# One encoder layer on one NeuronCore: the output projection of the second half interleaved, the first attention operands loaded ahead of the last key stores, the last RWKV pair among the last projections

## The chip, the cores and the metric

The kernel runs on one core of one Trainium2 chip. The core has TensorE (PE in the profile; PEld is its weight load), VectorE (DVE), ScalarE (ACT), GpSimd (POOL) and SyncE (SP), whose queue issues nearly all DMAs here. The metric is the device time of one execution in microseconds (us). Lower is better.

## What is computed

One layer of a streaming encoder, in fp32, for a prompt of 1024 frames and a sample of 64 frames that continues a past of 256 frames. The reference, cut to its skeleton:

```python
mod = silu(c) @ w_ada + b_ada                      # 6 x 1024 per sequence
sh1, sc1, gt1, sh2, sc2, gt2 = split(mod, 6)
h = rms_norm(x, norm1_g) * (1 + sc1) + sh1
proj = h @ w_in                                    # 1792 RWKV columns, 1544 FoX columns
# RWKV-7 group, 8 heads x 64: gates, delta-rule scan over time, group norm, bonus, gate
y_rwkv = ((groupnorm(scan(r, decay, k, v, kk, a, s0)) + bonus) * g)
# forgetting attention, 8 heads x 64: q, k normed; bias = difference of cumulated log forget
s = q @ k.T * 64**-0.5 + lc_q - lc_k               # causal mask, softmax
y_fox = softmax(s) @ v
x = x + gt1 * (concat(y_rwkv, y_fox) @ w_out)
h2 = rms_norm(x, norm2_g) * (1 + sc2) + sh2
x = x + gt2 * ((silu(h2 @ w_gate) * (h2 @ w_up)) @ w_down)     # 2816 wide
```

The outputs are x for both sequences, the RWKV states and shift rows, and the keys, values and log forget values of the new frames.

## The kernel before

**Halves and tiles.** The 1088 columns (frames) are worked on in two halves, called 0 (512 prompt frames) and 1 (512 prompt frames and the 64 sample frames, 576 in all). Activations lie with features on the partitions. Every large product is done in three fp32r matmuls: a weight and an activation are each split into a high part (`whi`, a cast on ACT) and a low part (`wlo`, a subtraction on DVE or on POOL, chosen by `pool_lo`), and high x high, high x low and low x high are added in PSUM (`mm3`). The weights come through a ring (`rraw` with four buffers of 512 KB, `whi` and `wlo` with two each).

**The order.** The program is written in one order, which serves as priority. A planner in the tile framework then lays out each engine's queue by what it takes to be ready, so that the queues mix stages where it finds room. On the chip each queue goes in its fixed order. A tile that takes over the space of another waits for that one's last user.

**The stages:**

1. Conditioning: 48 tiles of `w_ada`, each eight small matmuls, a copy on ACT, a transpose and a reduction on DVE (`ada_mm`, `ada_fin`). The first 16 come before anything else, the other 32 are dealt out one per projection (`background`).
2. `phase` for half 0, then half 1, in the order of the string `ORDER`. Z, D, A, B and N are the steps of one of four RWKV head pairs: Z projects, A builds the chunk matrices, B (`rwkv_b`) inverts them and runs a chain of 8 or 9 chunks, N norms and stores. Q, K and V project, q and k norm and store to DRAM scratch (`qx`, `kx`, `vscr`; `put_split` does the key and query stores), C puts the cached keys there, L makes the log forget rows. A pair whose B or N is not in the string is done "late": half 0's pair 3 at T3 and U3 in half 1's string, half 1's pair 3 after the phase.
3. Attention (`attend`) of half 0, head after head, in units that are staggered by a pipeline (`Pipe`). Each head first loads its operands `qs`, `q2`, `k1`, `k2`, `vs` from the scratch into one of two sets of tiles, by eight or nine DMAs. The sets lie in the pool `attp` and are shared by both halves. Then attention of half 1, with the output projection of half 0 dealt out between heads (`outproj`, po in the trace).
4. Squares of half 0's residual (`x1_sq`), the norm (`x1_rs`) and the FFN's operands of half 0 (`h2_make`, all of it), then the eight output tiles of half 1, each with its square; from output 5 on the first pair of "gate" weights is loaded and, at 6, prepared (`fast_raw`, `fast_prep`); then the "up" pair is loaded, and half 1's norm made.
5. The FFN in 22 steps (a weight pair of gate, then of up) of two passes each, half 0 and half 1. A pass (`fast_half`) is a Strassen-like product of seven groups of 12 matmuls. Hooks after each group carry on the preparation of the next weights (`STEPS`), half 1's `h2_make` (in the first pass) and, in the last pass, `mid`: the loads and splits of the first activations for the down projection.
6. The down projection (`down`): six groups of activations, eight output tiles each, with a weight split per tile (48 in all) on POOL, since `pool_lo` is set to True ahead of attention.

In the order of the program, B3 and N3 of half 1 stand here, after the whole string, and the operand tiles are made after them in space that the phase's work tiles held:

```python
hst.close()
fxs.close()
for b, f in late.values():
    f(b())
```

## Time and profile before

| | us |
|---|---|
| median of 3 runs | 1759.51 |
| lowest, highest | 1754.32, 1764.12 |
| the profiled execution, as timed | 1761.91 |
| its span in the profile | 1760.2 |
| mean granted clock of TensorE | 0.974 |

The span runs from the first to the last instruction. Busy time of an engine is the time in which one of its instructions runs; matmuls overlap in the pipeline, so that a busy PE isn't PE at its peak. A row of a stage table gives the stretch, its length, the busy time of PE, PEld, DVE, ACT and POOL with their numbers of instructions, the granted clock of TensorE (1.00 is full speed), the busy share of the 16 DMA engines and GB/s. A row in order of time gives start, duration, engine, line, operation, tiles and the number of instructions merged into it; in square brackets stands how long the engine had been idle, and what released it. A row of a group gives line, engine, operation, tiles and number, busy time and the mean of one in ns, then idle time before it and what ended it. SPq is SyncE's queue of DMA issues.

### The profile page before, as it was taken

To read this page: it belongs to the slowest core of one execution; us is meant where nothing else is said; L and a number is where in the kernel's file an instruction comes from. 1 tells how busy PE (TensorE), PEld (TensorE's weight loads), DVE (VectorE), ACT (ScalarE), POOL (GpSimd) and SP (SyncE) were. 2 spreads that over 40 slices of the span, in tenths; PEclk is the share of its full clock that TensorE was granted. 3 is DMA by queue.
4 is the path that set the end of the run, shared out by engine and by line. 5 is a ranking of instruction groups with operands and counts; after the bars stand their busy time and mean duration, and the time that the engine had idled before them with its cause. 6 is when DMAs were issued, how large, how long until landed. Compare 5 with 4: busy or idle time off the path is not lost.

```text
span 1760.2 us, 33567 instructions
## 1 busy us (share of the span) xinstructions
PE 1673.6 (95%) x12893; PEld 1454.0 (83%) x12893; DVE 1105.8 (63%) x2518; ACT 728.0 (41%) x1532; POOL 267.6 (15%) x468
## 2 busy tenths in 40 slices
PE   5999999999999998889999779999999999999999
PEld 3676666688888886666888779999999999999998
DVE  6676676757786753777876685556666654444434
ACT  4435454543555344566776363233333222112110
POOL 2102121121222122100212300000000000222221
PEclk9999999999999997889999899999999999999999
DMA  8435356642233336376663302222222224533313
GB/s 314 151 87 157 116 165 195 184 122 71 76 75 92 107 84 167 96 203 166 158 188 128 106 34 83 74 74 74 74 74 78 79 89 134 182 99 93 99 36 120
DMA packets 136143, 207.10 MB, mean 118 GB/s; under 512 B 64687, under 2 KB 72911, under 8 KB 135983
## 3 DMA queue, kind: packets, MB, share of 16 engines
q1 hardware_dynamic: 135982, 204.95, 39.1%
q8 instruction: 102, 1.67, 0.4%
q14 instruction: 59, 0.48, 0.1%
HBM read 157.65 MB, written 47.25 MB: 116 GB/s over the span
## 4 chain that ended last, share of the span: by engine, by line
PE 81%; DVE 7%; ACT 6%; issue 3%; DMA 3%; POOL 1%; SPq 0%; ACTq 0%; DVEq 0%; POOLq 0%
PE pd L1244 15%; PE pfc L1143 7%; PE pfe L1143 7%; PE pfa L1143 7%; PE pmm L294 5%; PE pmm L296 5%; PE pmm L295 5%; PE pfb L1143 4%; PE pav L952 2%; PE pbs L375 2%; PE ppt L930 2%; PE pA L464 2%; PE pS L613 1%; PE po L295 1%; PE po L294 1%
## 5 line engine op out<-in xcount | busy, mean ns | idle before, releaser
L216 POOL TENSOR_TENSOR wlo<-wraw,whi 128x512 fp32r<-128x512 f32 (+2 forms) x64 | 107.1, 1675 | 777.5 <-ACT whi L212 772.2
L294 PE MATMUL pmm<-hhi,whi 128*128 128x288 f32 (+1 forms) x624 | 220.3, 353 | 1.0 <-ACT pb L317 0.7
L295 PE MATMUL pmm<-hlo,whi 128*128 128x288 f32 (+1 forms) x624 | 216.8, 347 | 1.4 <-DVE hlo L272 1.4
L296 PE MATMUL pmm<-hhi,wlo 128*128 128x288 f32 (+1 forms) x624 | 215.6, 345 | 0.0
L212 ACT CAST whi<-wraw 128x1024 fp32r<-128x1024 f32 (+2 forms) x116 | 99.2, 855 | 234.8 <-PE pd L1244 168.1
L1244 PE MATMUL pd<-ah,whi 128*128 128x512 f32 (+1 forms) x528 | 173.3, 329 | 2.2 <-ACT ah L212 2.2
L1244 PE MATMUL pd<-al,whi 128*128 128x512 f32 (+1 forms) x528 | 174.1, 330 | 0.5 <-DVE al L216 0.5
L1244 PE MATMUL pd<-ah,wlo 128*128 128x512 f32 (+1 forms) x528 | 173.7, 329 | 0.0
L1248 DVE SCALAR_TENSOR_TENSOR x1t<-pd,mod,x1t 128x512 f32<-128x512 f32 x192 | 90.6, 497 | 132.1 <-PE pd L1244 131.0
L294 PEld LDWEIGHTS pmm<-hhi,whi 128*128 128x128 f32 x624 | 119.2, 191 | 14.3 <-ACT pb L317 2.5
L295 PEld LDWEIGHTS pmm<-hlo,whi 128*128 128x128 f32 x624 | 119.4, 191 | 11.1 <-DVE hlo L272 2.1
L296 PEld LDWEIGHTS pmm<-hhi,wlo 128*128 128x128 f32 x624 | 119.4, 191 | 10.2 <-issue 1.2
L1143 PE MATMUL pfc<-hh,hS 128*128 128x256 f32 (+1 forms) x352 | 102.3, 291 | 8.0 <-ACT hh L1045 5.6
L1244 PEld LDWEIGHTS pd<-ah,whi 128*128 128x128 f32 x528 | 99.8, 189 | 10.5 <-ACT ah L212 2.7
L1244 PEld LDWEIGHTS pd<-al,whi 128*128 128x128 f32 x528 | 99.8, 189 | 8.5 <-DVE al L216 0.7
L1244 PEld LDWEIGHTS pd<-ah,wlo 128*128 128x128 f32 x528 | 99.9, 189 | 7.5
L604 POOL TENSOR_SCALAR sd<-sv,pc 64x64 f32<-64x64 f32 x136 | 72.1, 530 | 202.7 <-DVE sv L617 190.3
L1143 PE MATMUL pfc<-hl,hS 128*128 128x256 f32 (+1 forms) x352 | 102.4, 291 | 0.0
L1143 PE MATMUL pfc<-hh,lS 128*128 128x256 f32 (+1 forms) x352 | 102.2, 290 | 0.0
L1143 PE MATMUL pfa<-hh,whi 128*128 128x256 f32 (+1 forms) x352 | 102.0, 290 | 0.0
L1143 PE MATMUL pfa<-hl,whi 128*128 128x256 f32 (+1 forms) x352 | 101.8, 289 | 0.0
L1143 PE MATMUL pfa<-hh,wlo 128*128 128x256 f32 (+1 forms) x352 | 101.4, 288 | 0.0
(360 smaller groups left out, 4471.6 us busy)
## 6 DMA issues: line engine op xcount, KB each, us to landing
wraw<-in_w_in_dram SPq DMA_DIRECT2D x52, 512.0 KB
wada<-in_w_ada_dram SPq DMA_DIRECT2D x48, 512.0 KB
as<-actscr SPq DMA_DIRECT2D x22, 544.0 KB
wraw<-in_w_gate_dram SPq DMA_DIRECT2D x22, 512.0 KB
wraw<-in_w_up_dram SPq DMA_DIRECT2D x22, 512.0 KB
wraw<-in_w_down_dram SPq DMA_DIRECT2D x40, 256.0 KB
wraw<-in_w_out_dram SPq DMA_DIRECT2D x16, 512.0 KB
actscr<-sg SPq DMA_DIRECT2D x22, 288.0 KB
```

Source lines behind the costliest of these rows:

```text
L212: nc.scalar.copy(hi, src)
L216: eng.tensor_tensor(lo, src, hi.bitcast(F32), op=ALU.subtract)
L294: nc.tensor.matmul(ps[0:M, 0:n], whi[:, k, 0:M], xhi[:, k, off:off + n], start=(k == 0), stop=False)
L295: nc.tensor.matmul(ps[0:M, 0:n], whi[:, k, 0:M], xlo[:, k, off:off + n], start=False, stop=False)
L296: nc.tensor.matmul(ps[0:M, 0:n], wlo[:, k, 0:M], xhi[:, k, off:off + n], start=False, stop=(k == kt - 1))
L375: nc.tensor.matmul(ps[:, 0:n], w, x[:, off:off + n], start=True, stop=True)
L464: nc.tensor.matmul(pa[h][:, i], kb[hp, c + i], rk[hp, c + i], start=True, stop=True)
L604: nc.gpsimd.tensor_scalar(sd[hsl[h]], sv[hsl[h], c, h], pc[hsl[h], c], None, op0=ALU.mult)
L930: nc.tensor.transpose(pt[0:rows, b - b0, t * P:t * P + qn], p[0:qn, b * P:b * P + rows], self.ident[0:qn, 0:qn])
L1143: nc.tensor.matmul(ps, l[:, k], r[:, s, k], start=(first and k == 0 and y == 0), stop=(k == 3 and y == 2), skip_group_check=True)
L1244: nc.tensor.matmul(ps[:, 0:n], w[:, i], x[:, t:t + n], start=(i == 0 and y == 0), stop=(i == len(fs) - 1 and y == 2))
L1248: nc.vector.scalar_tensor_tensor(dst, ps[:, so - off:so - off + l], self.mod[:, 40 + o, b:b + 1], dst, op0=ALU.mult, op1=ALU.add)
```

## The change

- `ORDER` of half 1 gets `P B3` ahead of the last `K2 k3 k2 V3`. P closes the RWKV work pools (now a stack of their own, `rws`, on the left, while the attention side's pools `fxs` move to the right), makes operand tiles for half 0 in their place (`at0`) and issues the 16 loads of heads 0 and 1. B3 then runs in the phase; N3 stays late.
- Half 0 and half 1 have operand tiles of their own (`att_ops`, `att_load`).
- The sample's new keys stand ahead of its cached keys in `kx`, so that a half's 576 columns are stored by one DMA in place of two; mask and transposes follow that order.
- `pool_lo` is set to False ahead of the squares of half 0: the low parts of the weights in half 1's output projection and in the down projection are made on DVE.
- The first two `w_out` weights of half 1 are loaded and split ahead of half 0's `h2_make`, whose steps are dealt out between half 1's outputs.
- The conditioning tiles 40 to 47, needed only in the down projection, are taken from the projections: 40 to 43 run after half 1's outputs, 44 to 47 in `gap`, between half 0's and half 1's first pass. The "up" weights are loaded there too, and prepared during half 1's first pass.
- The activations 0 and 1 for the down projection are loaded one weight pair earlier (`early` in `ffn`), 2 and 3 at the start of the last pass.

The diff, cut to its core:

```diff
-         "... V0 Q2 q2 K3 N2 Q3 q3 K2 k3 k2 V3")
+         "... V0 Q2 q2 K3 N2 Q3 q3 P B3 K2 k3 k2 V3")
...
             for h in range(2):
                 t = (self.kx if is_k else self.qx)[2 * j + h, r:r + 64]
-                hs = slice(64 * h, 64 * h + 64)
-                nc.sync.dma_start(t[:, t0:t0 + m], x[hs, 0:m].bitcast(F32))
-                if n > m:
-                    c = SP + PAST if is_k else SP
-                    nc.sync.dma_start(t[:, c:c + SS], x[hs, 512:576].bitcast(F32))
+                nc.sync.dma_start(t[:, t0:t0 + n], x[64 * h:64 * h + 64, 0:n].bitcast(F32))
...
+    def att_ops(self, pools, hf):
+        nq, nk, nb = (640, SP + PAST + SS, 11) if hf.smp else (512, 512, 4)
+        ops = [[p.tile(s, F32R, name=f"{n}x{i}") for n, s in (("qs", [P, nq]), ("q2", [68, nq]), ("k1", [P, nk]),
+                                                               ("k2", [68, nk]), ("vs", [P, nb, P]))]
+               for i, p in enumerate(pools)]
...
+        self.ops[hf.i] = ops
...
+        if hd > 1 or hf.smp:
+            self.att_load(hd, hf)
...
-    def outproj(self, hf, o, tags=("mm",)):
-        wh, wl = self.load_w(self.A["w_out"][o], [P, KT, P])
+    def outproj(self, hf, o, tags=("mm",), w=None):
+        wh, wl = w or self.load_w(self.A["w_out"][o], [P, KT, P])
...
+                def prep(x):
+                    for _ in range((0, 0, 0, 3, 2, 2, 1)[x] if i == 0 else self.STEPS[hf.i][x]):
+                        next(gen, None)
...
                 if i == 0 and hf.i == 0:
                     for _ in h2gen:
                         pass
+                    gap()
+                    raw.append(self.fast_raw(src[2]))
+                    gen = self.fast_prep(raw[1], nw)
...
-            self.background = [lambda t=t: self.ada_fin(self.ada_mm(t)) for t in range(16, 48)]
+            self.background = [lambda t=t: self.ada_fin(self.ada_mm(t)) for t in range(16, 40)]
...
+            def early():
+                rws.close()
+                p = E(at0, "att0")
+                self.att_ops([p, p], halves[0])
+                for hd in range(2):
+                    self.att_load(hd, halves[0])
...
+            self.pool_lo = False
             acc = None
             for o in range(KT):
                 acc = self.x1_sq(halves[0], o, acc)
-            for _ in self.h2_make(halves[0], self.x1_rs(halves[0], acc)):
-                pass
+            w1 = [self.load_w(A["w_out"][o], [P, KT, P]) for o in range(2)]
+            h2 = self.h2_make(halves[0], self.x1_rs(halves[0], acc))
...
             for o in range(KT):
-                self.outproj(halves[1], o, ("ab", "ce")[o % 2])
+                self.outproj(halves[1], o, ("ab", "ce")[o % 2], w1[o] if o < 2 else None)
                 acc = self.x1_sq(halves[1], o, acc)
+                next(h2, None)
+                if o in (0, 2):
+                    next(h2, None)
+                if o == 4:
+                    raw.append(self.fast_raw(pair("w_gate")))
                 if o == 5:
-                    raw.append(self.fast_raw(pair("w_gate")))
-                if o == 6:
                     for _ in self.fast_prep(raw[0], w):
                         pass
-            raw.append(self.fast_raw(pair("w_up")))
+            for _ in h2:
+                pass
+            ada = [(t, self.ada_load(t)) for t in range(40, 44)]
             rs = self.x1_rs(halves[1], acc)
...
+            def gap():
+                ada_run(ada[4:])
+                raw.append(self.fast_raw(pair("w_up")))
+            ada_run(ada)
+            ada += [(t, self.ada_load(t)) for t in range(44, 48)]
...
+            def early():
+                h2s[2].close()
+                self.spool.pools["as"] = L(early_s, "sas0", 2)
+                for f in range(2):
+                    pre.append(self.act_load(f, None))
...
             def mid(x):
                 if x == 0:
...
-                if x in (0, 1):
-                    pre.append(self.act_load(x, apools[0]))
-                if x in (3, 4):
-                    pre[x - 3] = self.act_split(pre[x - 3])
-                    pre.append(self.act_load(x - 1, apools[0]))
...
+                    for f in range(2, 4):
+                        pre.append(self.act_load(f, None))
...
+                if 0 < x < 5:
+                    pre[x - 1] = self.act_split((pre[x - 1][0], apools[0]))
```

More of the change, by code (lines that the diff above doesn't have):

```diff
@@ L87, in consts @@
         nc.vector.reciprocal(sg, sg)
-        self.ct = self.cmid.tile([P, KT, 32], F32, name="ct")
+        self.ct = c.tile([P, KT, 32], F32, name="ct")
         nc.gpsimd.memset(self.ct, 0.0)
@@ L703, in logf @@
         if hf.smp:
-            order += [(5, True, SP, P, None), (6, False, SP + P, P, None), (4, False, SP + PAST, SS, SP)]
+            order += [(5, True, SP + SS, P, None), (6, False, SP + SS + P, P, None), (4, False, SP, SS, SP)]
         acc = self.lacc
@@ L852, in att_pools, with att_load @@
         nc.vector.tensor_copy(self.cmask, cm)
[L853 to L861 removed]
+    def att_ops(self, pools, hf):
[3 more added lines that the diff above has]
+               for i, p in enumerate(pools)]
+        if hf.smp:
+            for qs, q2, _, _, _ in ops:
+                for t in (qs, q2):
+                    self.nc.gpsimd.memset(t[:, 576:640].bitcast(F32), 0.0)
+        self.ops[hf.i] = ops
+    def att_load(self, hd, hf):
         nc = self.nc
[L864 to L867 removed]
+        qs, q2, k1, k2, vs = self.ops[hf.i][hd % 2]
         n, t0 = hf.n, hf.t0
@@ L906, in unit @@
                     c += w
-                nc.tensor.matmul(pq[0:qn, nk - qn:nk], self.identb[0:qn, 0:qn], self.cmask[0:qn, 0:qn], start=False,
+                cm = 0 if smp else nk - qn
+                nc.tensor.matmul(pq[0:qn, cm:cm + qn], self.identb[0:qn, 0:qn], self.cmask[0:qn, 0:qn], start=False,
                                  stop=True, skip_group_check=True)
@@ L1157, in fast_half, with ffn @@
                 h(x)
-    def ffn(self, halves, raw, w, h2gen, mid):
+    def ffn(self, halves, raw, w, h2gen, gap, early, mid):
         nc, A = self.nc, self.A
@@ L1168, in ffn @@
             p, up = i // 2, i % 2
-            if i + 2 < len(src):
+            if i and i + 2 < len(src):
                 raw.append(self.fast_raw(src[i + 2]))
+            if i == len(src) - 2:
+                early()
             old, nw = gen, {}
-            gen = self.fast_prep(raw[i + 1], nw) if i + 1 < len(src) else iter(())
+            gen = self.fast_prep(raw[i + 1], nw) if 0 < i < len(src) - 1 else iter(())
             for hf in halves:
@@ L1302, in phase @@
                 self.cache_kv(j)
+            elif op == "P":
+                self.early()
             elif op == "S":
@@ L1433, in run @@
             self.spool.pools.update({"fs": L(mix0, "sfs", 2)})
+            self.att_ops([R(att, f"attp{i}", 1) for i in range(2)], halves[1])
             PB = lambda es, name, b: E(es, name, b, space=PSUM, reuse_waits="tile")
```

87 lines of the change are left out of this document (46 added, 41 removed).

## The prediction

> **What bounds the kernel now.** I read the page first: the span, the busy shares and the chain that ended last.
>
> ```profile
> span 1760.2 us, 33567 instructions
> ...
> PE 1673.6 (95%) x12893; PEld 1454.0 (83%) x12893; DVE 1105.8 (63%) x2518; ACT 728.0 (41%) x1532; POOL 267.6 (15%) x468
> ...
> PE 81%; DVE 7%; ACT 6%; issue 3%; DMA 3%; POOL 1%; SPq 0%; ACTq 0%; DVEq 0%; POOLq 0%
> ```
>
> TensorE (PE) is busy for 95% of the span and makes up 81% of the chain, so only the holes in PE are worth anything, together with the slices in which its granted clock falls. Next I took the busy time by stage, with bounds that I set where the work changes. The columns are the stretch, its length, the busy time of PE, PEld, DVE, ACT and POOL, the granted clock, the DMA share and GB/s.
>
> ```profile
> 60.00:440.00 380.00, 366.97 (x3118) 273.60 (x3118) 263.51 (x728) 176.48 (x386) 69.09 (x156) 0.97 0.47 135
> ...
> 660.00:683.00 23.00, 22.73 (x297) 19.58 (x297) 8.85 (x15) 13.35 (x26) 5.19 (x5) 1.00 0.52 144
> 683.00:717.00 34.00, 26.05 (x157) 19.83 (x149) 10.54 (x39) 10.11 (x34) 7.03 (x18) 0.52 0.45 119
> 717.00:745.00 28.00, 25.83 (x148) 19.00 (x147) 22.84 (x73) 19.05 (x59) 5.64 (x20) 0.97 0.44 123
> 745.00:780.00 35.00, 28.62 (x166) 20.44 (x166) 28.84 (x88) 25.58 (x79) 3.91 (x20) 1.00 0.63 178
> 780.00:815.00 35.00, 30.05 (x129) 22.14 (x129) 21.98 (x43) 19.16 (x40) 0.34 (x2) 0.80 0.77 219
> ...
> 940.00:1011.00 71.00, 57.80 (x404) 56.05 (x404) 50.62 (x66) 34.09 (x47) 24.40 (x7) 0.93 0.41 134
> 1011.00:1035.00 24.00, 14.35 (x101) 12.95 (x101) 20.00 (x34) 22.04 (x35) 0.00 (x0) 0.95 0.03 13
> 1035.00:1480.00 445.00, 444.98 (x3514) 444.69 (x3514) 267.15 (x507) 135.99 (x253) 1.66 (x1) 0.99 0.24 75
> 1480.00:1500.00 20.00, 17.25 (x106) 15.76 (x105) 10.76 (x15) 6.43 (x7) 1.82 (x1) 0.92 0.89 292
> 1500.00:1757.00 257.00, 256.92 (x1555) 234.29 (x1553) 113.76 (x207) 44.47 (x63) 57.86 (x46) 1.00 0.32 101
> ```
>
> The FFN (1035 to 1480) and the down projection (1500 to 1757) are full and can give nothing. Four places are not: 683 to 780 (last RWKV pair, then attention of half 0), 940 to 1011 (output projection of half 1), 1011 to 1035 (norm of half 1) and 1480 to 1500 (turn to the down projection). The change works on just these.
>
> **Part 1: pair 3 of half 1 (B3) among the last projections, first attention operands loaded ahead.** I looked at the order of time on PE and on SP's queue.
>
> ```profile
> 624.58 0.46 PE L597 MATMUL pR<-sv,At 128*128 128x128 f32 x2
> ...
> 652.17 0.46 PE L597 MATMUL pR<-sv,At 128*128 128x128 f32 x2
> ...
> 679.35 0.59 PE L523 MATMUL pg<-gt,At 32*32 32x32 f32 x25
> ...
> 699.37 0.77 PE L597 MATMUL pR<-sv,At 128*128 128x128 f32 x2 [0.36 <-DVE sv L617]
> ...
> 703.65 0.77 PE L597 MATMUL pR<-sv,At 128*128 128x128 f32 x2 [0.36 <-DVE sv L617]
> ...
> 705.48 0.77 PE L902 MATMUL psc<-k1x,qsx 128*128 128x256 f32 x2
> ```
> ```profile
> 659.54 0.34 SPq L625 DMA_DIRECT2D out_state_s_dram<-state  x1
> ...
> 663.26 0.60 SPq L800 DMA_DIRECT2D qx<-shi  x1
> ...
> 692.36 0.42 SPq L870 DMA_DIRECT2D qsx<-qx  x1
> ```
>
> B3 begins at 679.35, when the projections are used up, and runs alone: one chunk takes 703.65 - 699.37 = 4.28 us, with a granted clock of 0.52. Pair 2, among projections, took (652.17 - 624.58) / 7 = 3.94 us for a chunk while PE was filled by other work. The loads for the first two attention heads are issued from 692.36 on, behind a row of stores of 0.6 us each, and the first score matmul comes at 705.48. After the change those 16 loads (eight a head) stand ahead of K2, k3, k2 and V3 and need only half 0's rows, long since written; the space they load into is that of the RWKV work tiles, whose last user is A3. B3 can begin once pair 2's state is out (659.54), with two projections left to fill its gaps, and attention once the last projection has read the activations, near 685.
>
> The worth by PE's work: 660 to 780 holds 22.73 + 26.05 x 0.52 + 25.83 + 28.62 = 90.7 us of PE at full clock. The 22.7 of projections run at the share of their row, 0.99. The other 68 run at the share of attention beside a chain (25.83 / 28 = 0.92), or at that of attention alone (28.62 / 35 = 0.82): 23 + 74 = 97 us or 23 + 83 = 106 us, for 120 now. So 14 to 23 us, and I take **18**, the middle, as both kinds of stretch remain. The low end for the range is 0 (attention starts where it did); a loss is excluded only if SP does not hold weight loads behind the 16 issues that come early, 16 x 0.6 = 10 us at worst. The 16 are moved, not added. The single store for 576 columns takes away 32 issues at 0.6 us, 19 us of SP's time; it is costed at nothing beyond this, since PE at 0.99 covers the stores until 683. The new order of the sample's keys moves columns only: nothing.
>
> **Part 2: outputs of half 1 interleaved, weight splits on DVE.** The waits of PE from 940 to 1011 and from 1011 to 1041, in us in total, times, longest; then DVE's splits in the projections and ACT in order of time:
>
> ```profile
> PE po L296 <- POOL wlo L216: 10.2, 2, 8.8
> ...
> PE pfc L1143 <- ACT hh L1045: 5.6, 1, 5.6
> PE pfc L1143 <- DVE fu L1153: 2.3, 1, 2.3
> ```
> ```profile
> L216 DVE TENSOR_TENSOR wlo<-wraw,whi 128x1024 fp32r<-128x1024 f32 x47 | 57.3, 1219 | 22.2 <-ACT whi L212 21.3 <-DMA dm<-At 0.6
> ```
> ```profile
> 1012.35 1.28 ACT L1185 ACT_TABLE_LOAD   x1
> 1013.64 0.38 ACT L1185 ACTIVATE sg<-pfa 128x256 f32<-128x256 f32 x1
> 1014.04 1.28 ACT L1015 ACT_TABLE_LOAD   x1
> ...
> 1016.25 1.28 ACT L1016 ACT_TABLE_LOAD   x1
> ```
>
> The steps that prepare a pair of weights on DVE, in the stretch 940 to 1045:
>
> ```profile
> L1086 DVE TENSOR_TENSOR wraw<-wraw 128x512 f32<-128x512 f32 x8 | 5.5, 682 | 0.1
> ```
>
> PE lost 10.2 us to two POOL splits; a split on DVE takes 1.22 us. `pool_lo = False` puts all of them on DVE, two weights are split before the norm of half 0, and that norm is dealt out between outputs. What is late next is DVE: its 50.62 us plus 8 x 1.22 = 9.8 us is 60.4 us, and PE's own work is 57.8. The stage of 71 us can shrink to about 61, a gain of **10**. Ends: 13.2 (all of PE's idle time) and 0 (DVE in the place of POOL).
>
> Then comes the norm of half 1, for which PE waits in the other two rows (5.6 and 2.3 us). Three table loads (3 x 1.28 = 3.84 us) lie between its last square and its scaling, because half 0's first Silu got ahead. In the new order half 0's first FFN pass starts later, so I count half, **2** (0 to 3.84). The "up" weights are now loaded in the gap and prepared inside half 1's first pass, where none were before; the preparation is 1.22 us plus nine steps of 0.68 us, 7.3 us, on a DVE that has half 1's norm ahead of it. I estimate **-3**, somewhat under half of it (0 to -7.3). The part gives 9.
>
> On the table loads: the Trainium skill ("ScalarE: Activation LUTs", What ACT_TABLE_LOAD costs) adds a drain of about 1.38 us to each switch, 2.66 us in all. The trace does not agree: the Silu at 1013.64 begins 0.01 us after its load has ended. By the page the three would be 8.0 us, and the sum 2 us lower.
>
> **Part 3: eight of the conditioning tiles (40 to 47) moved.** They leave the projections and stand around half 0's first pass. All of their matmuls, then the transposes, from 60 to 440 (30 tiles; busy time of PE and PEld):
>
> ```profile
> 60.00:440.00 380.00, 24.41 (x480) 13.28 (x480) 0.97 0.47 135
> ```
> ```profile
> 60.00:440.00 380.00, 8.51 (x30) 4.33 (x30) 0.97 0.47 135
> ```
> ```profile
> L200 DVE TENSOR_REDUCE mred<-pada x48: 145/158/167, 16.2 to 437.3; 128x2 f32<-128x8 f32 x48
> ```
>
> One tile is (24.41 + 8.51) / 30 = 1.10 us of busy PE, so 8.8 us for eight at most; since neighbours overlap I take 6 (0 to 8.8), with PE there at 366.97 / 380. In their new place they cost the same PE time, covered by the 24 - 14.35 = 9.65 us of idle PE in 1011 to 1035. Without that cover they cost up to 8.8. On DVE, the tight engine there, they add 8 x 0.16 = 1.3 us; I take 1. Net **5**. Their eight 512 KB loads go through the same four weight buffers on SP's queue, and the "up" pair stands behind them; DMA is at 0.03 in that stage, and the wait is in the -3 above.
>
> **Part 4: activations for the down projection loaded earlier.** PE idles 20 - 17.25 = 2.75 us, in the chain behind two loads:
>
> ```profile
> 1479.99 5.29 DMA as<-actscr
> ...
> 1487.77 6.46 DMA as<-actscr
> ```
>
> Tiles 0 and 1 now load one weight pair earlier, and 2 and 3 at the start of the last pass. The clock of 0.92 over 20 us is 1.6 us more. Bounds 0 and 4.4; I take **4**, as the loads have a whole pass of cover.
>
> **Part 5: the rest.** Half 1's attention has operand tiles of its own. PE idles 35 - 30.05 = 4.95 us from 780 to 815, mostly for pipeline refill; I take **1** (-2 to 4.95). The down projection's 48 splits of 128x512 move to DVE: 48 x 0.68 = 33 us on a DVE that is busy for 113.76 of 257 us. ACT and DVE there:
>
> ```profile
> 1500.94 0.63 ACT L212 CAST whi<-wraw 128x512 fp32r<-128x512 f32 x1 [1.63 <-PE pd L1244]
> ...
> 1501.03 0.64 DVE L1248 SCALAR_TENSOR_TENSOR x1t<-pd,mod,x1t 128x224 f32<-128x224 f32 x2 [1.90 <-PE pd L1244]
> ...
> 1506.92 0.62 ACT L212 CAST whi<-wraw 128x512 fp32r<-128x512 f32 x1 [3.91 <-PE pd L1244]
> ```
>
> One tile lasts 1506.92 - 1500.94 = 6 us, and with two weight buffers a split has that long. So nothing. If DVE takes them late, that is the first rival.
>
> **Sum.** 18 + 9 + 5 + 4 + 1 = 37 us. The profiled execution took 1761.91 us in all, 1.7 us more than its span; 1761.9 - 37 = 1725. The median of the runs, 1759.51, lies 2.4 us under it: **1722 us**.
>
> **Rivals.**
> - *DVE holds the splits back (slower).* In the down projection an evacuation of 0.64 us and a split of 0.68 us would lie between a tile's last matmul and the next tile's third, with two matmuls of 257 / 1555 = 0.17 us over them: 1.0 us of stall in 48 tiles, and 0.64 + 1.22 - 0.33 = 1.5 us in the eight of the output projection, 60 us in all. 1722 + 60 = 1782. It makes the kernel slower from 37 / 56 = 0.7 us a tile on. Against it: the 47 splits on DVE above stood in projections with PE at 0.97 to 1.00. For it: DVE now also carries the evacuations there. The Trainium skill ("TensorE: Matmul & The Clock Gate", Architectural detail) calls DVE strict FIFO: a split waiting for its load holds all behind it. No row here shows that in this stage.
> - *Attention does not start earlier.* Its work tiles lie where the activations and the last stores' tiles were; if the last stores hold them, the 18 goes to 0: 1740. For it: stores run until 692. Against: the loads, not the tiles, are seen to come last.
> - *DVE takes POOL's place in the output projection.* 60.4 us of DVE in 61 leaves no slack; without the 9, 1731.
> - *The change doesn't do what it says.* The order on each engine is planned, not written: the score matmul at 705.48 stands among B3's though written after it. If B3 and the norms land where they were, only parts 3 and 4 remain: 1759.5 - 9 = 1750.
>
> **How the numbers follow.** Forecast 0.70; rivals in order 0.06, 0.10, 0.08, 0.06. With all high bounds (23 + 17 + 8 + 4.4 + 5 = 57) it is 1702; the second and third rival lie at 1740 and 1731, both of them at 1749. The range is 1700 to 1745. A measurement tells 0.5%, 8.8 us, from no change: faster 0.88 (forecast, second and third), same 0.06 (the last), slower 0.06 (the first).
>
> **What would show it.** Part 1: score matmuls by about 690, the clock at 1.00 from 683 to 717, half 0's attention ended near 762. Part 2: no PE wait on POOL, half 1's first FFN pass some 9 us sooner after half 0's attention than now, at most one table load ahead of its norm, a wait for prepared "up" weights near 3 us. Part 3: 40 conditioning tiles by 440 in place of 48, and the projections there some 6 us shorter. Part 4: no wait on activations at the turn. The prediction falls if the clock still drops after the projections, or if PE waits on DVE splits in the down projection.

## The result, and the profile after

The changed kernel takes **1739.15 us** (median; 1735.78 to 1744.26) beside 1761.82 for the kernel before on the same chip, a ratio of 0.989 (95% interval 0.986 to 0.992). In a second session it took 1742.5 us beside 1757.67, ratio 0.991 (0.989 to 0.993). By these medians it is faster by 23 and by 15 us, some 40 to 60% of the 37 us that the prediction summed up. Every later ratio is to the kernel before on the same chip in the same session. The changed kernel's profile begins so:

```profile
span 1734.2 us, 33257 instructions
...
PE 1663.8 (96%) x12893; PEld 1447.9 (83%) x12893; DVE 1126.6 (65%) x2574; ACT 729.1 (42%) x1532; POOL 180.8 (10%) x412
...
PE 82%; DVE 7%; ACT 7%; DMA 2%; issue 2%; SPq 1%; POOL 0%; DVEq 0%; ACTq 0%; POOLq 0%
```

PE bounds it as before. The stage that Part 1 is about, by the bounds of the prediction's table (stretch, length, busy PE, PEld, DVE, ACT, POOL, granted clock, DMA share, GB/s):

```profile
660.00:683.00 23.00, 22.76 (x329) 18.31 (x328) 10.05 (x21) 14.44 (x33) 5.21 (x7) 1.00 0.54 140
683.00:717.00 34.00, 30.76 (x220) 25.16 (x219) 23.27 (x79) 22.53 (x68) 11.57 (x27) 1.00 0.52 151
717.00:745.00 28.00, 24.35 (x151) 18.41 (x150) 24.83 (x79) 21.45 (x66) 4.39 (x18) 1.00 0.63 179
745.00:780.00 35.00, 29.54 (x146) 21.59 (x147) 25.14 (x65) 23.57 (x61) 2.24 (x13) 0.85 0.66 191
780.00:815.00 35.00, 32.60 (x164) 23.96 (x162) 22.62 (x46) 18.66 (x42) 3.37 (x7) 0.90 0.72 186
```

From 683 to 717 us the clock is 1.00 where it was 0.52, and the first score matmul comes at 692.48 us in place of 705.48: this went as told. The loss against the forecast lies earlier. I counted the projection matmuls (`pmm`, 1872 in both halves) and cut both traces at the 1056th, the 1152nd and the 1632nd. Before, then after:

```profile
447.27:484.75 37.48, 36.88 (x456) 30.99 (x455) 27.77 (x56) 20.93 (x49) 10.22 (x20) 1.00 0.23 51
484.75:617.98 133.23, 130.71 (x1275) 112.76 (x1273) 95.59 (x253) 61.30 (x148) 28.54 (x61) 1.00 0.35 91
```
```profile
437.30:482.02 44.72, 43.04 (x450) 35.25 (x449) 29.02 (x64) 19.73 (x45) 10.16 (x18) 0.89 0.19 43
482.02:623.34 141.32, 138.38 (x1307) 119.39 (x1306) 98.97 (x262) 65.04 (x155) 31.99 (x65) 0.98 0.33 87
```

With eight conditioning tiles fewer, matmul 1056 comes 10 us sooner (437.30 for 447.27). Then the way to matmul 1632 takes 186.0 us in place of 170.7, at a clock of 0.89 and 0.98 where it had been 1.00, and there the changed kernel is 5.4 us late. Not all of these 15.3 us are the clock: 17 us at 0.50 can cost PE 8.5 us at most, and four `pbs` and four `plora` matmuls, 3 to 4 us by the times of their records, now stand behind matmul 1056 and stood ahead of it before. From matmul 1632 to the last matmul of attention the changed kernel gains 20.0 us, to the end of the output projection 8.3 more, and to the end 3.1.

### The profile page after: what moved, and what is told of

It reads as the page before. It is cut to its first block, busy times and chain, and to the rows that moved or that the text cites. A ratio compares the mean times of both kernels' runs of the same rounds, so it can differ in the third digit from the quotient of the medians.

```text
span 1734.2 us, 33257 instructions
## 1 busy us (share of the span) xinstructions
PE 1663.8 (96%) x12893; PEld 1447.9 (83%) x12893; DVE 1126.6 (65%) x2574; ACT 729.1 (42%) x1532; POOL 180.8 (10%) x412
## 4 chain that ended last, share of the span: by engine, by line
PE 82%; DVE 7%; ACT 7%; DMA 2%; issue 2%; SPq 1%; POOL 0%; DVEq 0%; ACTq 0%; POOLq 0%
PE pd L1264 15%; PE pfc L1153 8%; PE pfe L1153 8%; PE pfa L1153 7%; PE pmm L294 5%; PE pmm L296 5%; PE pmm L295 5%; PE pfb L1153 4%; PE pav L962 2%; PE pbs L375 2%; PE pA L464 2%; PE ppt L940 2%; PE po L294 1%; PE po L295 1%; PE po L296 1%
## 5 line engine op out<-in xcount | busy, mean ns | idle before, releaser
L216 DVE TENSOR_TENSOR wlo<-wraw,whi 128x1024 fp32r<-128x1024 f32 (+2 forms) x108 | 103.8, 961 | 26.0 <-ACT whi L212 25.6
```

The costliest lines, as they stand in the source:

```text
L216: eng.tensor_tensor(lo, src, hi.bitcast(F32), op=ALU.subtract)
```

## The experiments

**Part 3 alone, both ways.** Undone in the changed kernel:

```diff
-            self.background = [lambda t=t: ... for t in range(16, 40)]
+            self.background = [lambda t=t: ... for t in range(16, 48)]
```

with `ada_run` and its loads taken out; and, in the kernel before, done alone: `range(16, 40)`, tiles 40 to 47 after half 1's outputs and ahead of the "up" load.

> The changed kernel with its conditioning tiles 40 to 47 back among the projections; all else as changed. Theory A (these tiles were filler: without them half 1's run of 32x32 matmuls falls between projections at another place, the clock is halved at about 459 us and the stretch from 437 to 623 us is 15 us longer): projection matmul number 1632 ends near 618 to 620 us instead of 623, no granted clock under 0.95 from 447 to 500 us, time 1734 us or less, 5 us under the changed kernel. Theory B (the 15 us come from another edit or from chance, and the eight tiles were worth their 5 us as forecast): number 1632 at 628 us or later, time about 1744 us.

> The kernel before with one edit: conditioning tiles 40 to 47 taken out of the projections and computed after half 1's output projection. Theory A: projection matmul number 1056 comes 7 to 10 us sooner than before, number 1632 not sooner or up to 5 us later, with the clock under 0.95 after 447 us; time 1762 to 1770 us. Theory B: number 1632 comes 6 us sooner, the clock stays at 1.00 there, and the time is about 1757 us.

With the tiles back: 1735.13 us, ratio 0.985 (0.983 to 0.987). With the tiles moved alone: 1764.77 beside 1760.18, ratio 1.003 (1.002 to 1.005). Theory A both times, with the first time 1 us over what it named; matmul 1632 came even later in the second kernel than it allowed (627.63, 10 us after the 617.98 of the kernel before). Same stretches, tiles back, then moved alone:

```profile
446.05:483.56 37.51, 36.89 (x456) 30.98 (x455) 27.80 (x56) 20.96 (x49) 10.26 (x20) 1.00 0.23 52
483.56:617.27 133.71, 130.98 (x1292) 113.31 (x1291) 94.37 (x253) 61.99 (x149) 30.39 (x63) 1.00 0.35 91
```
```profile
444.28:488.54 44.26, 42.76 (x451) 35.24 (x449) 28.48 (x63) 19.76 (x45) 9.47 (x18) 0.88 0.18 42
488.54:627.63 139.09, 136.40 (x1307) 117.55 (x1306) 98.82 (x262) 65.19 (x155) 31.48 (x65) 1.00 0.34 88
```

The tiles' edit carries the slow stretch with it into the kernel before, and takes it out of the changed one. Forecast as a gain of 5 us, Part 3 is a loss of 4 to 7 us by the medians of e1 and of the changed kernel, which ran on other chips, and of 7 to 11 by the two ratios; e2 says 3 to 8.

**What halves the clock.** In the planned order, half 1's first clump of 32x32 matmuls (B0) falls between other projections once the tiles are gone: 107 of its 126 (two records each in the trace) into one group of 12 projection matmuls, where it was spread as 27, 80 and 18 over three. Two orders and a dial:

```diff
-... Z1 K0 D1 U3 B0 A1 D2 ...
+... Z1 K0 D1 U3 A1 B0 D2 ...      # e9: A1 ahead of B0
-... D0 A0 L Z1 K0 D1 ...
+... D0 A0 L K0 Z1 D1 ...          # e10: K0 ahead of Z1
-range(16, 40)
+range(16, 44)                     # e5: four tiles moved, 44 to 47
```

> The changed kernel with only the last four of the eight conditioning tiles (44 to 47) out of the projections; the other four are background there again. If the halved clock follows from how late in half 1's projections the first clump of 32x32 matmuls falls, the dip near 460 us is there again and the time is about 1739 us, as in the changed kernel. If it follows from how dense the clump is between projections (in the planned order it is spread over three times as many of them here as in the changed kernel), the clock stays at 1.00 from 437 to 482 us, projection matmul number 1632 comes by 619 us, and the time is 1733 to 1736 us.

> The changed kernel, all eight conditioning tiles moved, with one pair of steps exchanged in half 1's order: A1 ahead of B0. In the planned order the first clump of 32x32 matmuls then falls as 35, 36, 45 and 9 into four successive groups of 12 projection matmuls, in place of 107 and 18 in two. If the dense clump halves the clock (and the tiles only moved it there), the dip near 460 us is gone, projection matmul number 1632 comes by 617 us, and the time is 1730 to 1735 us. If the loss comes from the tiles being gone as such, the dip stays within 10 us of that place and the time at 1737 to 1742 us.

> The changed kernel, all eight tiles moved, with K0 ahead of Z1 in half 1's order. In the planned order the first clump comes some 60 projection matmuls sooner and falls as 72, 27 and 27 into three groups of 12. By the density theory the dip near 460 us is gone or shorter (72 is less than 107), and the time 1732 to 1738 us; by the theory that the missing tiles themselves cost it, the clock falls again within 15 us of the clump's end and the time stays at 1737 to 1742 us.

Four moved: 1734.4 us (ratio 0.985), with no stretch of half clock between 430 and 538 us. A1 ahead of B0, all eight moved: no half clock between 418 and 762 us, and matmuls 1056 to 1632 take 172.1 us, nearly the 170.7 of the kernel before:

```profile
448.28:478.50 30.22, 29.11 (x387) 24.69 (x385) 24.82 (x50) 14.40 (x28) 4.42 (x12) 1.00 0.25 60
478.50:620.38 141.88, 140.26 (x1336) 121.49 (x1334) 101.71 (x275) 70.61 (x170) 30.99 (x68) 1.00 0.32 86
```

So the dip near 460 us comes with the clump's density, not with the tiles being gone as such. All twenty profiles say the same: the eleven with 107 or more of the clump in one group have a dip that begins between 459 and 466 us, the nine with 80 or fewer have none there. The time with A1 ahead of B0, 1738.86 us (0.984 to 0.991), is nevertheless over what was expected and no better than the changed kernel's: this profile has 48 us at half clock ahead of 440 us and 24 us from 660 to 840. K0 ahead of Z1 took the dip near 460 us away as well, and others came at 430, 529 and 618 us: 1745.99 us, worse than expected.

**A view of the clock itself.** At the dip, then in the same clump of the kernel before (3.41 us each, the step in which the record of the granted clock changes; in the kernel before the record's own steps lie 0.2 us ahead of these rows):

```profile
449.15:452.56 3.41, 3.41 (x26) 3.12 (x25) 3.41 (x6) 1.86 (x5) 0.61 (x2) 1.00 0.38 141
452.56:455.97 3.41, 3.41 (x103) 2.86 (x102) 2.43 (x5) 0.00 (x0) 0.00 (x0) 1.00 0.21 77
455.97:459.38 3.41, 3.41 (x130) 3.02 (x126) 3.02 (x8) 1.09 (x4) 1.10 (x1) 1.00 0.03 5
459.38:462.79 3.41, 3.41 (x34) 2.98 (x30) 3.38 (x6) 1.55 (x5) 2.60 (x4) 0.50 0.02 5
```
```profile
455.98:459.39 3.41, 3.41 (x77) 3.00 (x72) 3.27 (x6) 1.08 (x2) 0.03 (x1) 1.00 0.62 165
459.39:462.80 3.41, 3.41 (x152) 3.20 (x144) 3.06 (x7) 1.41 (x6) 0.61 (x2) 1.00 0.03 5
```

PE never idles here. What fills the changed kernel's window ahead of the dip (groups of PE: line, tile, shape, count, busy us, mean ns):

```profile
L523 PE MATMUL pu<-inv,g 32*32 32x32 f32 x72 | 1.7, 192 | 0.0
L523 PE MATMUL pw<-g,inv 32*32 32x32 f32 x22 | 1.0, 192 | 0.0
...
L296 PE MATMUL pmm<-hhi,wlo 128*128 128x288 f32 x1 | 0.4, 399 | 0.0
L295 PE MATMUL pmm<-hlo,whi 128*128 128x288 f32 x1 | 0.4, 397 | 0.0
L294 PE MATMUL pmm<-hhi,whi 128*128 128x288 f32 x1 | 0.3, 294 | 0.0
```

A 32x32 matmul uses 32 of 128 rows and of 128 columns. Weighted by that share of the array, the window streams 321 columns a us, and the one before it 561; the sparsest one in this clump of the kernel before streams 421, and the next is still granted 1.00. Unweighted, they stream 1350, 1396 and 1687. I did this sum for every 3.41 us window from 41 to 1724 us of all twenty profiles: of 69 windows under 300 weighted columns a us at full clock 68 were followed by half clock, of 1002 between 300 and 1000 147, of 8318 above 1000 none. Unweighted, 58 of 1876 windows between 1000 and 1500 were followed by it too. In between the sum does not decide for a single window: the windows ahead of the eleven dips stream 322 to 477, and others of 421, 429 and 443 near the clump (before, e18, e9) were not followed by one.

Wide matmuls added to the clump, their results overwritten, were to show this by addition:

```diff
+            if hf.i and j == 0:
+                for _ in range(3):      # ahead of each of the five groups of 32x32
+                    nc.tensor.matmul(pg[1] as 288 columns, self.hhi[:, 1, 0:P], self.hhi[:, 0, 0:288], ...)
```

> The changed kernel with 15 matmuls of 128x288 added among the 32x32 matmuls of half 1's first clump; their results are overwritten and go nowhere. By themselves they cost about 2 us of PE (15 by 0.13 us). If the clock is granted by how much of the array works and 32x32 matmuls count for little, the dip near 460 us is gone, the projections end some 3 us sooner, and the time is 2 to 4 us under the changed kernel's. If the clock follows PE's busy time or something else, the dip stays and the time is 2 us more.

It failed: 1743.85 us, and a dip of 13.7 us at 462.1 us. The additions lengthened the clump (the 96 projection matmuls take 50.0 us for 44.7) and did not stand evenly: 1287 weighted columns a us in the window at 455 us, then 467, and then half clock. What is shown is that the clump's arrangement brings this dip or takes it away. That the clock follows the share of the array at work fits the count over all windows, and is not shown by adding work.

**Part 1: order or place?** Four versions of the end of half 1's string, and then the operand tiles' place:

```diff
-Q3 q3 P B3 K2 k3 k2 V3
+Q3 q3 P K2 k3 k2 V3        # e3: B3 late
+Q3 q3 B3 K2 k3 k2 V3 P     # e4: loads last
+Q3 q3 K2 k3 k2 V3 P        # e6: both as before
```

> The changed kernel with the last pair's chain (B3) again after the last projections, the operand loads of the first two heads still ahead of K2, k3, k2 and V3. If the interleaved chain carries the gain of this stage, the chain runs alone again, the clock falls after 680 us and the time rises by 10 to 15 us to about 1750 us or more. If the loads carry it, the first scores come by 693 us as in the changed kernel and the time stays within 4 us of 1739.

> The changed kernel with B3 among the last projections, but the operand loads issued after V3's stores. If the loads carry the gain of this stage, the first scores come at about 705 to 715 us and the time is 10 to 15 us over 1739. If the chain among the projections carries it, the time stays within 4 us of 1739 with the clock near 1.00 from 683 to 717 us.

> The changed kernel with the order of half 1 as before: B3 after the last projections and the operand loads issued after V3's stores (Part 1 undone, the rest kept). If Part 1 is worth the 18 us of the forecast, 1757 us. If each of its two halves alone gave most of it (each undone by itself cost 2 to 6 us), then no more than 8 us: 1747 us. First scores at about 705 to 715 us and the clock near 0.5 from 690 to 720 us in either case.

1741.41, 1744.68 and 1740.38 us; the ratios 0.989, 0.991 and 0.989 are those of the changed kernel. The string is worth nothing that these runs can tell. Even with the loads written last (e6), the planner issues the first one at 651.47 us, 46 us ahead of V3's stores, and the mean clock from 690 to 720 us is 0.94, where either theory had it near 0.5:

```profile
651.47 0.59 SPq L868 DMA_DIRECT2D qsx<-qx  x1
...
697.23 4.58 SPq L808 DMA_DIRECT2D vscr<-vs  x4
```

B3 then runs beside attention. In the changed kernel it does so too, though it is written among the projections: its inversions fall there (675 to 685 us), but its chain of chunks (`pR`) starts 2.5 us ahead of the last projection matmul and ends at 724 us, 5.7 us sooner than before. The start of the chain, the last projection matmul, the first score and the end of the chain:

```profile
689.70 0.46 PE L597 MATMUL pR<-sv,At 128*128 128x128 f32 x2
...
692.21 0.30 PE L296 MATMUL pmm<-hhi,wlo 128*128 128x288 f32 x1
...
692.48 0.36 PE L910 MATMUL psc<-k1x,qsx 128*128 128x256 f32 x1
...
724.06 0.39 PE L597 MATMUL pR<-sv,At 128*128 128x128 f32 x2
```

Next, the tiles back among the attention's pools (e11), and, in the kernel before, nothing but their new place (e14):

```diff
 # e11, on the changed kernel
-                p = E(at0, "att0")
-                self.att_ops([p, p], halves[0])    # and the two att_load
...
             self.att_pools(att, R)
+            self.att_ops([R(att, f"attp{i}", 1) for i in range(2)], halves[1])
+            self.ops[0] = self.ops[1]
```

e14 takes `fxs` (right), `rws`, `at0`, `att_ops` and `att_load` into the kernel before and calls `early()` after the whole string; B3, stores, splits and conditioning tiles stay as before.

> The changed kernel, with the operand tiles of half 0's attention back among the attention's own pools at the far end of the memory (where they were before, over space that the projections' last stores hold), and loaded by each head itself; B3 stays in the order. If the tiles' place is what lets the loads go early, the loads are issued after V3's stores, the first scores come at 705 us or later, and the time rises by 10 to 15 us to 1750 us or more. If shorter queues or B3 carry the gain, the first scores come by 695 us and the time stays within 4 us of 1739.

> The kernel before with one edit: the operand tiles of half 0's attention get a place of their own, in the space of the RWKV work tiles, and the first two heads' loads are written right after the last projection step; B3, stores, splits and conditioning tiles as before. If the place carries the gain of this stage alone, first scores by about 690 us, the clock at 0.8 or more from 685 to 719 us, and 12 to 20 us less than before: 1740 to 1748 us. If it needs the single stores or B3 in the order, first scores at 700 us or later and 1752 us or more.

The old place costs the whole gain: **1761.7 us**, ratio 1.0005 (0.999 to 1.002). The new place alone gives it: **1741.41 us**, ratio 0.991 (0.988 to 0.993). First loads and scores of e11 (SP's queue, then PE), and of e14:

```profile
703.16 4.38 SPq L808 DMA_DIRECT2D vscr<-vs  x4
707.59 0.58 SPq L868 DMA_DIRECT2D qsx<-qx  x1
```
```profile
719.33 0.77 PE L909 MATMUL psc<-k1x,qsx 128*128 128x256 f32 x2
```
```profile
643.46 0.53 SPq L871 DMA_DIRECT2D qsx<-qx  x1
```
```profile
683.69 0.39 PE L913 MATMUL psc<-k1x,qsx 128*128 128x256 f32 x1
```

**The single stores,** in two again (columns 0 to 511, then 512 to 575):

```diff
-nc.sync.dma_start(t[:, t0:t0 + n], x[64 * h:64 * h + 64, 0:n].bitcast(F32))
+for a, b in ((0, m), (m, n)):   # m = min(n, 512)
+    if b > a:
+        nc.sync.dma_start(t[:, t0 + a:t0 + b], x[64 * h:64 * h + 64, a:b].bitcast(F32))
```

> The changed kernel with each store of 576 columns of half 1's keys and queries again as two DMAs (512 and 64 columns), 32 issues more on SP, 19 us of its queue's time. The forecast costed the single store at nothing: the time stays within 4 us of 1739. Rival: SP's queue sets when the last stores and the next weights come, and the time rises by 5 to 10 us.

1753.03 us (1744.82 to 1757.48), ratio 0.996 (0.994 to 0.998): the rival's way, and more, 9 to 14 us over the changed kernel by ratios and medians. But the first scores come at 697.67 us, between the changed kernel's own 692.48 and 698.40 in its two profiles. The time goes after that: from the first score to the last matmul of attention it takes 240.9 us, where the changed kernel takes 229.0 and 230.0. The clock from 660 to 840 us is 0.90, where the changed kernel has 0.95 and 0.94, the new place alone 0.99, the old place 0.88 and the kernel before 0.87. The edit also changes PE's planned order: 918 of its 12893 matmuls, all but four of them between 520 and 920 us, stand at another place than in the changed kernel (10 do between the two profiles of the changed kernel itself). So whether SP's 19 us or the new order costs the time is not shown. Those rows, e12 first, then changed, e14, e11, before:

```profile
660.00:840.00 180.00, 163.62 (x1102) 128.13 (x1103) 119.15 (x313) 110.69 (x292) 29.07 (x77) 0.90 0.53 152
```
```profile
660.00:840.00 180.00, 164.23 (x1151) 126.90 (x1151) 125.85 (x329) 119.66 (x309) 31.65 (x78) 0.95 0.60 166
```
```profile
660.00:840.00 180.00, 159.91 (x1154) 123.91 (x1153) 128.75 (x330) 119.15 (x308) 27.63 (x75) 0.99 0.59 163
```
```profile
660.00:840.00 180.00, 158.13 (x1030) 119.92 (x1029) 109.31 (x294) 101.06 (x270) 27.71 (x72) 0.88 0.53 152
```
```profile
660.00:840.00 180.00, 157.28 (x1022) 119.50 (x1021) 112.98 (x295) 104.60 (x275) 25.89 (x71) 0.87 0.59 160
```

**Parts 2 and 4.** `pool_lo` left at True after attention; and `mid` as before, with `early` loading nothing:

> The changed kernel with the weight splits of half 1's output projection and of the down projection on POOL again; the outputs stay interleaved with the norm. Forecast's step: PE waits some 10 us on POOL in the output projection and the time is 1746 to 1749 us. Rival: the two weights split ahead of the norm already hide it, so only 0 to 3 us; in the down projection nothing changes (PE 257 of 257 us in both).

> The changed kernel with the activations of the down projection loaded and split as before, one tile at a step of the last pass. Forecast's step: PE waits some 3 us on activations at the turn, the clock dips there, and the time is 4 us over the changed kernel, 1743 us. Rival: the loads start from a free buffer earlier anyway, and it stays at 1739 us.

1744.16 us (ratio 0.991, 0.988 to 0.994) and 1745.68 us (0.992, 0.989 to 0.994): neither interval is clear of the changed kernel's, so the stages decide. From half 1's last attention matmul to its last output, before, changed, and with the splits on POOL:

```profile
935.80:1010.50 74.70, 61.50 (x418) 58.84 (x419) 50.62 (x66) 34.67 (x48) 25.82 (x8) 0.93 0.40 133
```
```profile
921.20:987.60 66.40, 60.20 (x419) 57.65 (x420) 50.38 (x73) 34.35 (x48) 1.43 (x1) 0.97 0.41 143
```
```profile
922.10:993.90 71.80, 61.97 (x421) 59.01 (x422) 52.61 (x66) 34.36 (x48) 18.97 (x8) 0.95 0.41 138
```

The splits on DVE give 5.4 of the 8.3 us in that stage. (e2 and e14, where it is as before, take 74.1 us; all other versions with both edits 64.9 to 67.4.) The down projection lasts 266.0 us with them there and 266.3 with POOL, so DVE holds nothing back. For Part 4, the down projection before, changed, with late activations (e8), and in e2 and e14, which load them exactly as before:

```profile
1489.90:1760.20 270.30, 264.27 (x1585) 240.28 (x1584) 119.17 (x215) 47.78 (x66) 57.86 (x46) 0.99 0.34 109
```
```profile
1468.20:1734.20 266.00, 262.68 (x1586) 239.59 (x1584) 139.02 (x258) 45.51 (x64) 0.00 (x0) 1.00 0.33 106
```
```profile
1474.50:1741.40 266.90, 263.16 (x1586) 239.62 (x1584) 141.18 (x261) 46.84 (x66) 0.00 (x0) 1.00 0.34 110
```
```profile
1497.60:1763.70 266.10, 262.77 (x1586) 239.57 (x1584) 119.12 (x214) 46.70 (x65) 57.10 (x46) 1.00 0.33 110
```
```profile
1471.60:1741.50 269.90, 264.37 (x1586) 240.33 (x1584) 119.09 (x215) 47.79 (x66) 57.77 (x46) 0.99 0.34 109
```

The old loading costs 0.9 us in e8 and 0.1 in e2, but 3.9 in e14 and 4.3 in the kernel before. In e14 the chain at the turn is the one that the prediction read, behind two loads, with PE waiting 2.4 us on the activations and a step of half clock at 1478 us:

```profile
1461.90 4.95 DMA as<-actscr
...
1469.33 6.27 DMA as<-actscr
```

So the loss at the turn comes in two of the four profiles with the old loading; in none of the sixteen with the new one, whose down projections last 265.4 to 266.3 us.

**The changed kernel again, other places, and a faster version.** First itself, in more runs; then the eight tiles computed in half 0's attention, one after each head, with A1 ahead of B0; then Part 3 and the string undone together; last, as that, with four tiles moved and A1 ahead of B0:

```diff
 # e16
                 pipe.run(self.attend(hd, halves[0]))
+                self.ada_fin(self.ada_mm(40 + hd, None, "ch"))
 # e17: range(16, 48), no ada_run;  "... Q3 q3 K2 k3 k2 V3 P"
 # e18: range(16, 44), ada = 44 to 47;  "... U3 A1 B0 D2 ... Q3 q3 K2 k3 k2 V3 P"
```

> The changed kernel itself, again. Theory A (the halved clock near 460 us belongs to its planned order): a dip of about 10 us near 460 us again, projection matmul number 1632 at 620 us or later, time 1736 to 1744 us. Theory C (the dip was chance in one profile): no dip between 450 and 480 us and number 1632 by 618 us. By either, dips at other places (near 346 or 406 us) may come or go.

> The changed kernel with the clump spread (A1 ahead of B0) and the eight conditioning tiles computed in half 0's attention, one after each head, in place of around half 0's first FFN pass. There PE idles some 17% between 692 and 800 us. If the tiles fit into those holes, the half-1 norm stage is 2 us shorter and attention no longer: 1733 to 1737 us. If DVE or the DMA queue of that stage is the tight resource, attention of half 0 is 5 us longer and the time 1740 us or more.

> The changed kernel with Part 3 undone (all conditioning tiles among the projections) and half 1's order as before (B3 and the loads last): the operands' place, single stores, the interleaved outputs, DVE splits and early activations are left. If these parts add to the place alone (1741 us) what the stages show (8 us in the output projection and 1 to 4 at the turn), 1730 to 1734 us. If B3 among the projections is needed beside them, the clock falls after 690 us and the time is 1738 us or more.

> As the run before it, but with four of the eight tiles moved and the first clump spread (A1 ahead of B0). If spread clumps keep the clock at 1.00 from 437 to 660 us and four tiles less are worth 3 us, 1728 to 1732 us; if the order costs as much elsewhere as it brings there, the time is that of the run before it, within 3 us.

First, 1742.5 us, again with a dip at 459.9 us (13.7 us long) and matmul 1632 at 628.2. Next, 1746.4 us, over what was forecast (from matmul 1632 to the last of attention it takes 316.0 us where e9 takes 303.6, and the norm stage saves 1.5). Then 1735.7 us (ratio 0.988, 0.984 to 0.992), somewhat over what was expected; and last **1727.17 us** (1722.6 to 1728.9), ratio **0.981** (0.979 to 0.984). The last one beats both kernels. Its clock is 1.00 from 440 to 660 us and 0.97 after:

```profile
442.97:476.98 34.01, 33.05 (x426) 28.09 (x425) 28.34 (x57) 15.62 (x32) 7.67 (x14) 1.00 0.25 54
476.98:610.52 133.54, 129.94 (x1168) 112.24 (x1166) 91.38 (x256) 68.38 (x165) 30.61 (x65) 1.00 0.34 88
...
660.00:840.00 180.00, 165.84 (x1193) 130.91 (x1191) 133.90 (x349) 122.46 (x321) 33.20 (x84) 0.97 0.59 163
```

A ledger over the profiles puts it together. Half the time that the clock record shows at 0.50, without the last stretch at the span's end, is an upper bound of what the slow clock takes from PE; the rest of the span is what remains.

| profile | span | half-clock loss | by 440 us | 440 to 660 | 660 to 840 | after 840 | rest of the span |
|---|---|---|---|---|---|---|---|
| before | 1760.2 | 46.1 | 11.9 | 0 | 23.9 | 10.2 | 1714.1 |
| new place alone (e14) | 1741.6 | 29.0 | 17.1 | 0 | 1.7 | 10.2 | 1712.6 |
| changed | 1734.2 | 32.4 | 10.2 | 8.5 | 8.5 | 5.1 | 1701.8 |
| changed, again (e13) | 1742.9 | 46.1 | 17.1 | 11.9 | 10.2 | 6.8 | 1696.8 |
| tiles back (e1) | 1730.8 | 32.4 | 13.7 | 0 | 13.7 | 5.1 | 1698.4 |
| old place (e11) | 1760.8 | 56.3 | 20.5 | 5.1 | 22.2 | 8.5 | 1704.5 |
| stores in two (e12) | 1752.1 | 52.9 | 18.8 | 5.1 | 18.8 | 10.2 | 1699.2 |
| place and outputs (e17) | 1736.7 | 41.0 | 17.1 | 5.1 | 10.2 | 8.5 | 1695.7 |
| four tiles, spread (e18) | 1720.9 | 23.9 | 15.4 | 0 | 5.1 | 3.4 | 1697.0 |

## Why the prediction was wrong, and what of it held

- **Part 3 is the term that was mis-sized: +5 forecast, -4 to -7 measured** (e1 against the changed kernel in its two sessions, by medians; -7 to -11 by ratios; e2 against before says -3 to -8). The 8.8 us of PE work did leave the projections. The step that failed is the silent one after it, that the rest of the phase stays as it is: the order is planned anew, the clump of 32x32 matmuls closes up, and the clock is halved at 459 us, where it had been 1.00. All but one of the fourteen profiles with eight tiles moved also show a dip between 403 and 411 us, which none of the four profiles with 48 tiles has.
- **Part 1 had the right size, 18 (e14 alone: 16.3, interval 12 to 21), and two wrong steps.** That loads were late and the clock fell meanwhile was right. But B3's chain did not move among the projections: the projections that were to fill its gaps ended 2.5 us after it had begun (689.70 us). And neither P's position nor B3's in the string moves the time. The place of the tiles does: in the old one the loads stand behind V3's stores (e11), in the new one the planner brings them forward by itself, wherever they are written (e6, e14). The prediction's rival "attention does not start earlier" named the place as what could undo the gain, and argued against it that the loads come last, not the tiles; it was the tiles' place that made them come last. That the single stores are worth nothing did not hold either: undone in the changed kernel they cost 9 to 14 us. Yet e14 keeps them in two and has its whole 16, so this price belongs to the one planned order.
- **Part 2's outputs came as told** (8.3 us for 10). The 2 us for table loads did not come: half 0's Silu still gets ahead, and three loads stand in that norm as before; PE waits 4.4 us for `hh` there in place of 5.6. The 3 us of waiting for "up" weights did not come either, no wait for them shows. From the last output to the down projection the stage is 1.2 us longer (480.6 for 479.4; 482.5 in the second profile).
- **Part 4 had its mechanism right and took a loss that comes only sometimes for one that is always there:** 4 forecast; 3.9 to 4.3 in two profiles with the old loading, 0.1 to 0.9 in two others. By these four it is worth some 2 us.
- **Part 5's 1 us is too small to be told from the rest.** The splits on DVE in the down projection cost nothing, as told; the first rival did not happen.
- **With the measured sizes the sum comes out:** 16.3 for the place, 8.3 - 1.2 for the outputs and what follows, 0 to 4 for the turn, less 4 to 7 for Part 3, is 16 to 24 us, beside 23 and 15 measured. That the parts add this well is partly luck, since stores and dips depend on the order. By the ledger, work outside slow stretches fell by 12 to 17 us. The slow stretches, 46.1 us before, should have lost the 17 us of the one that began at 684 us and come to 29, as in e14; they came to 32.4 and 46.1, since new ones appeared from 440 to 660 and, in the second profile, by 440 us. The prediction's own sign for a failure, a clock that drops after the projections, looked at the wrong end of the phase.

What stays open: e17, without Part 3 and the string, lies at 1735.7 us, no better than e1; its parts save 17 us outside the slow stretches against e14, and 12 of them are lost to new dips. Why dips come at just those places I did not settle.

## What to carry to other kernels

Where a planner orders the queues, look at what a moved step stood between before counting its own time as gain, and compare the planned order around small matmuls in both kernels. When a load comes late, ask first whose space it lands in; a place of its own can do alone what a new order can't. A loss seen in one profile, such as a dip of the clock at one turn, goes into a sum only with its share: more profiles of versions that leave that stage alone tell how often it comes.

## What the runs showed of the hardware

- The granted clock changes in steps of 3.413 us, and every stretch at 0.50, but for one at the end of the span, is a whole number of them. Half clock followed windows in which little of the array worked: 68 of 69 below 300 weighted columns a us, 147 of 1002 up to 1000, none above. PE can be busy for all of such a window: 32 windows with PE busy throughout were followed by half clock, all of them between 314 and 853 weighted columns a us.
- The Trainium skill ("TensorE: Matmul & The Clock Gate", What's actually happening) speaks of a free-running window of about 3.4 us, whose phase at a kernel's start differs from run to run. The profiles agree: counted from the start of the span, the steps' phase was 2.01 and 2.58 us in the two profiles of the changed kernel, 1.82 in before, 0.95 in e1, 0.43 in e2, 3.06 in e18. A sparse place of 4 us may fill one window or be split over two, which fits dips that come and go between profiles of one program (near 346 us: in the changed kernel's second profile, not in its first). The table in that section of the Trainium skill halves the clock after an idle window; here PE was not idle but ran mostly 32x32 matmuls back to back.
- Two stores in place of one, 32 DMA issues more on one queue, made the changed kernel 9 to 14 us slower, most of it at half clock (half-clock loss 52.9 us for 32.4 and 46.1, the rest of the span the same within 3 us); the planned order changed with them, so that the queue's part in it is not shown.
